# Two edits in a hybrid encoder kernel: the retention scores of two heads in one product over 128 rows, and another way of counting filler products

## The chip, the cores and the metric

The kernel runs on one core of a Trainium2 chip. The metric is the device time of one execution in microseconds (us), the median of several runs. A core has a matrix engine (TensorE, PE in the rows; its weight loads are PEld), a vector engine (VectorE, DVE), a scalar engine (ScalarE, ACT), GpSimd (POOL) and SyncE (SP), each with an instruction stream of its own; semaphores tie them together. All names of tiles in the rows are the program's own.

## What is computed

Two layers of an encoder over 512 prompt frames and 32 sample frames (544 columns, handled as two halves of 272). In every layer four token mixers read one residual stream: stick-breaking attention (sb), retention (ret), forgetting attention (fox) and sparse attention chosen by an indexer (dsa). Their outputs are gated, summed, projected, normalised, and a SwiGLU network follows. The change touches the retention, of which this is the part that matters (four heads of 64):

```
scores = einsum('bnhd,bmhd->bhnm', q, k) * decay[None]
o = einsum('bhnm,bmhe->bnhe', scores, v)
o = o + einsum('bnhd,bhde->bnhe', q, state) * exp((n + 1) * log_gamma)
state = exp(c * log_gamma) * state + einsum('bmhd,bmhe->bhde', k_dec, v)
y_ret = head_norm(o) * silu(g)
```

## The kernel before

Feature-major tiles hold two heads in the 128 partitions: of `q` and `k` (names `rq` and `rk` in the rows, shape 128 x 2 x 544) index p is the pair of heads, and partitions 0 to 63 and 64 to 127 are its heads s = 0 and s = 1. The prompt's 512 frames are taken in four chunks of 128. For each chunk, and for each s, the kernel takes a PSUM bank `z` and multiplies 64 rows of `k` with 64 rows of `q`, once for each pair p (line 1612); VectorE multiplies by the decay into `A` (line 1613). Then come the state (`S`, from the decayed keys `kd`), the product of `S` with the decayed queries `qd`, the product of `A` with the values `rvt`, and a normalisation over each head (`oc`, `st`, `mv`, `rs`). These products are in float32, and TensorE runs each of them as two passes, which are two rows of the trace. The large products (names `wop`, `whi`, `wlo`, `wb` with `T`, `h0hi`, `q`, `yhi`) are split into parts of one pass each.

Order and places are not written by hand. The program is recorded as a list of operations; `Plan.schedule` simulates five engines with estimated durations and lets the operation of the smallest number go first on every engine; `Memory` then assigns SBUF addresses by the times so found, tries four settings (`FITS`) and keeps the one that ends first. An additional tile or another estimated duration can so change addresses, and by them waits and the order, in places far from the edit.

`Plan.fillers` puts filler products into the holes that TensorE has in this plan: a product of 128 columns of the constant tile `idle`, into an unused part of PSUM bank 0 (line 657). They are there to keep TensorE active. Before each operation the number is limited by two things: the hole in front of it less 0.1 us, and what is missing to a share of activity over a trailing stretch (the two constants of `WARM`); a filler counts 0.056 us. The activity of an operation was the time that the plan gives it. All operations are issued at line 659, so the rows carry this line for everything but fillers.

Of the kernel before, what the change touches and what calls it, by code (L numbers as in the profile page):

```python
# [11 lines left out]
F32 = mybir.dt.float32  # L12
F32R = mybir.dt.float32r
BF = mybir.dt.bfloat16
AF = mybir.ActivationFunctionType
OP = mybir.AluOpType
# [5 lines left out]
T = 512  # L22
# [306 lines left out]
class Plan:  # L329
# [305 lines left out]
    def fillers(self, order):  # L635

        share, width = self.WARM
        count, busy, end = {}, [], 0.0
        for i in sorted((i for i in order if self.ops[i].eng == "PE"), key=lambda i: self.ops[i].start):
            op = self.ops[i]  # L640
            s = op.start
            busy = [(a, b) for a, b in busy if b > s - width]
            done = sum(b - max(a, s - width) for a, b in busy)
            n = int(min(share * width - done, s - end - 0.1) / self.IDLE_MM) if end else int(s / 2 / self.IDLE_MM)
            if n > 0:
                count[i] = n
                busy.append((end, end + n * self.IDLE_MM))
            end = s + op.dur
            busy.append((s, end))
        return count  # L650

    def issue(self, order):
# [12 lines left out]
class Build:  # L665
# [875 lines left out]
    def retention(self):  # L1541
        nc, l = self.nc, self.l
        cs = self.fm("cs")
        a, b = CONST_AT["cos"][0], CONST_AT["sin"][1]
        nc.sync.dma_start(cs.rearrange("p a b -> p (a b)"), self.consts_dram[:, a:b])
        q = self.rotary(self.proj(COL["ret_q"], "rq0"), cs)
        k = self.rotary(self.proj(COL["ret_k"], "rk0", 0.125), cs)
# [12 lines left out]
        for c in range(2):  # L1560
            a = COL["ret_g"] + c * 128
            raw = self.load([(self.i["w_in"][l][:, a:a + 128], 0, 128)], 8)
            self.dense(raw, 0, 128, 8, self.hx,
                       lambda h, ps: silu(c, h, ps))
        y = self.fm("y_ret")
        dec = self.const("dec").rearrange("m (s p n) -> m s p n", s=2, p=2)
        qdt = self.const("qdec").rearrange("r (p n) -> r p n", p=2)
        op, os_ = self.outs["ret_state"]
# [36 lines left out]
        for c in range(4):  # L1605
            cc = slice(c * 128, (c + 1) * 128)
            A = self.w512("A", (128, 2, 2, 128))
            for s in range(2):
                r = slice(s * 64, s * 64 + 64)
                z = self.tps("rz")  # L1610
                for p in range(2):
                    nc.tensor.matmul(z[:, p * 128:(p + 1) * 128], k[r, p, cc], q[r, p, cc], start=True, stop=True)
                nc.vector.tensor_tensor(A[:, s], z[:, :256].rearrange("m (p n) -> m p n", p=2), dec[:, s], op=OP.mult)
            kd = kdecay(c * 128, 128, "kdec")
            self.select(SELECT[2])
            N = state_from(S, kd, v[:, c], 128, "g128")
            if c:
                qd = self.w512("qd", (128, 2, 128))
                nc.gpsimd.tensor_tensor(qd, q[:, :, cc], qdt, op=OP.mult)
            o = self.aps("ro")  # L1620
            for p in range(2):
                if c:
                    nc.tensor.matmul(o[:, p * 128:(p + 1) * 128], qd[:, p], S[:, p], start=True, stop=False)
                for s in range(2):
                    h = 2 * p + s
                    nc.tensor.matmul(o[:, h * 64:(h + 1) * 64], A[:, s, p], v[:, c, h * 64:(h + 1) * 64],
                                     start=not c, stop=not c or s == 1)
            self.head_norm_T(o, 128, sg, y, c * 128)
            S = N
# [8 lines left out]
        z = self.tps("rzs")  # L1638
        for p in range(2):
            nc.tensor.matmul(z[:32, p * 64:(p + 1) * 64], k[:, p, T:NT], qb[:, p].rearrange("r s q -> r (s q)"),  # L1640
                             start=True, stop=True)
        A = self.w512("As", (128, 2, 2, 32))
        nc.vector.tensor_tensor(A[:32].rearrange("m p s n -> m s p n"),
                                z[:32, :128].rearrange("m (p s n) -> m s p n", p=2, s=2), dec[:32, :, :, :32],
                                op=OP.mult)
# [5 lines left out]
        o = self.aps("ros")  # L1651
# [436 lines left out]
```

## Time and profile before

| | us |
|---|---|
| median of 3 runs | 1942.51 |
| lowest and highest of them | 1942.05, 1944.62 |
| the profiled execution's own time | 1938.36 |
| its span, first to last instruction | 1936.6 |
| mean granted TensorE clock in the profiled execution | 0.995 of full speed |

A profile page shows one execution: busy time of each engine, a strip of 40 slices, the chain of work that ended last, and groups of equal instructions. Behind it a trace can be asked for single instructions in order of time, for what ended the idle time before one, and for the busy times in chosen stretches. In a timeline row a merged run of equal instructions has one start, one length, a count, and in brackets the idle time before it and the operation that ended it. The length of a product includes its way through the array, so the distance of two starts tells what it occupies, and two lengths that overlap are normal.

### The profile page before, as it was taken

What the parts mean: (1) busy time and instruction counts of PE and PEld (TensorE: products, weight loads), DVE (VectorE), ACT (ScalarE), POOL (GpSimd) and SP (SyncE); (2) the same over time, 40 slices, a digit from 0 to 9 for tenths busy, and PEclk for the clock granted to TensorE, in tenths of its full rate; (3) what the DMA queues carried; (4) which work ended last, traced back from release to release, by engine and by line L of the source; (5) the groups of instructions that cost most, each with busy time, mean ns of one, the idle gap of its engine ahead of it and who ended that gap; (6) DMA issues with size and microseconds to landing.
All of it is one profiled execution on the core that took longest, in us unless ns stands there. A gap on an engine that the chain in (4) does not pass through costs nothing.

```text
span 1936.6 us, 39257 instructions
## 1 busy us (share of the span) xinstructions
PE 1871.6 (97%) x14658; PEld 1815.8 (94%) x14658; DVE 1607.1 (83%) x3566; ACT 1053.3 (54%) x2183; POOL 498.8 (26%) x500
## 2 busy tenths in 40 slices
PE   9999999999999999999999999999999999999997
PEld 8998898999999999999989989999999999999996
DVE  5988768887879989988789796687788799899875
ACT  4465533555637656556465563365556475565552
POOL 0343031143441111321413421312434301114101
PEclk9999999999999999999999999999999999999999
DMA  8222243667542587776413222346665237777741
GB/s 229 79 64 81 55 101 75 153 142 163 145 124 77 135 195 174 170 180 169 130 23 95 60 84 68 78 107 159 151 154 155 86 86 169 188 174 175 171 114 47
DMA packets 387423, 241.38 MB, mean 125 GB/s; under 512 B 27272, under 2 KB 363576, under 8 KB 386976
## 3 DMA queue, kind: packets, MB, share of 16 engines
q1 hardware_dynamic: 361888, 193.78, 36.2%
q0 software_dynamic: 25344, 45.10, 13.8%
q8 instruction: 115, 1.88, 0.4%
q14 instruction: 76, 0.62, 0.1%
HBM read 183.69 MB, written 7.82 MB: 99 GB/s over the span
## 4 chain that ended last, share of the span: by engine, by line
PE 71%; DVE 17%; DMA 5%; ACT 4%; issue 3%; POOL 1%; SPq 1%; POOLq 0%; ACTq 0%; DVEq 0%
PE bank L659 70%; DVE wop L659 3%; DMA ws<-wa 3%; DVE lnw L659 2%; DVE y L659 2%; DVE wsum L659 1%; DVE wlo L659 1%; DVE st L659 1%; DVE q L659 1%; DVE score L659 1%; DVE fu L659 1%; SPq L659 1%; DVE su L659 0%; DVE sv L659 0%; ACT wop L659 0%
## 5 line engine op out<-in xcount | busy, mean ns | idle before, releaser
L659 PE MATMUL bank<-T,wop 128*128 128x272 f32 x3456 | 460.6, 289 | 4.6 <-DVE su L659 3.1
L659 PEld LDWEIGHTS bank<-T,wop 128*128 128x128 f32 x3456 | 443.3, 188 | 7.1 <-DVE su L659 4.3
L659 PE MATMUL bank<-h0hi,wop 128*128 128x272 f32 x1152 | 244.9, 291 | 0.3 <-DVE acc L659 0.3
L659 PEld LDWEIGHTS bank<-h0hi,wop 128*128 128x128 f32 x1152 | 190.0, 188 | 3.6 <-DVE acc L659 0.5
L659 POOL DMA_DIRECT2D wt<-raw x88 | 76.6, 870 | 370.8 <-DVE wop L659 68.2
L659 POOL DMA_DIRECT2D ws<-wa x88 | 76.9, 874 | 352.7 <-DVE wop L659 114.8
L659 ACT ACTIVATE wop<-raw 128x512 fp32r<-128x512 f32 (+1 forms) x176 | 108.9, 620 | 107.1 <-PE bank L659 96.2
L659 PE MATMUL bank<-h0lo,wop 128*128 128x272 f32 x576 | 165.7, 288 | 0.0
L659 PE MATMUL bank<-q,wop 128*128 128x272 f32 x1176 | 153.0, 290 | 4.4 <-DVE su L659 2.6
L659 PEld LDWEIGHTS bank<-q,wop 128*128 128x128 f32 x1176 | 148.8, 189 | 7.5 <-DVE su L659 3.6
L659 DVE TENSOR_TENSOR wop<-raw,wop 128x512 fp32r<-128x512 f32 (+1 forms) x176 | 126.0, 718 | 31.1 <-ACT wop L659 30.5
L659 ACT ACTIVATE wop<-wsum 128x512 fp32r<-128x512 f32 (+1 forms) x176 | 109.1, 620 | 73.7 <-PE bank L659 46.5
L659 PE MATMUL bank<-h0hi,whi 128*128 128x272 f32 (+1 forms) x480 | 146.0, 304 | 2.3 <-ACT h0hi L659 2.3
L659 DVE TENSOR_TENSOR wlo<-raw,whi 128x1024 fp32r<-128x1024 f32 (+1 forms) x92 | 123.7, 1351 | 27.8 <-PE bank L659 12.7
L659 PE MATMUL bank<-h1hi,whi 128*128 128x272 f32 (+1 forms) x480 | 142.3, 296 | 1.1 <-DVE iq L659 1.1
L659 ACT ACTIVATE whi<-raw 128x1024 fp32r<-128x1024 f32 (+1 forms) x92 | 95.5, 1049 | 87.2 <-PE bank L659 46.6
L659 PE MATMUL bank<-h0hi,wlo 128*128 128x272 f32 (+1 forms) x480 | 139.3, 290 | 2.0 <-DVE wlo L659 2.0
L659 PE MATMUL bank<-h0lo,whi 128*128 128x272 f32 (+1 forms) x480 | 139.2, 290 | 2.0 <-DVE h0lo L659 2.0
L659 DVE TENSOR_TENSOR wop<-wsum,wop 128x512 fp32r<-128x512 f32 (+1 forms) x176 | 122.2, 694 | 22.8 <-ACT wop L659 22.0
L659 PE MATMUL bank<-h1lo,whi 128*128 128x272 f32 (+1 forms) x480 | 138.5, 289 | 0.5 <-DVE h1lo L659 0.5
L659 PE MATMUL bank<-h1hi,wlo 128*128 128x272 f32 (+1 forms) x480 | 138.6, 289 | 0.0
L659 PE MATMUL bank<-h1hi,wop 128*128 128x272 f32 x576 | 121.4, 289 | 0.0
(452 smaller groups left out, 5076.7 us busy)
## 6 DMA issues: line engine op xcount, KB each, us to landing
raw<-in_w_in_dram SPq DMA_DIRECT2D x46, 512.0 KB, 3.8
ws<-wa POOLq DMA_DIRECT2D x80, 256.0 KB, 4.4
wt<-raw POOLq DMA_DIRECT2D x80, 256.0 KB, 4.0
raw<-in_w_ffn_in_dram SPq DMA_DIRECT2D x76, 256.0 KB, 3.6
raw<-in_w_in_dram SPq DMA_DIRECT2D x68, 256.0 KB, 3.5
wa<-in_w_ffn_in_dram SPq DMA_DIRECT2D x38, 256.0 KB, 3.5
ws<-in_w_ffn_in_dram SPq DMA_DIRECT2D x38, 256.0 KB, 2.9
wt<-in_w_ffn_in_dram SPq DMA_DIRECT2D x38, 256.0 KB, 4.2
```

Source lines behind the costliest of these rows:

```text
L659: call(*a, **k)
```

## The change

It has two parts. First, a tile `qm` (128 x 2 x 2 x 512, float32) is made once in each layer, after the rotary step: for head s it holds that head's 64 rows of `q` in their own partitions, and zeros in the other 64. GpSimd writes the zeros (two operations), ScalarE copies the rows (two operations). The scores of both heads of a pair are then one product over all 128 rows with 256 columns, and one bank takes all four heads; the multiplication by the decay stays in two operations, which now read this bank. Second, the activity of an operation in `Plan.fillers` becomes the number of its streamed columns over 2400 a microsecond (float32 counts twice) spread over its planned time, in place of that time itself; the limit by the hole and the length of a filler stay.

```diff
         count, busy, end = {}, [], 0.0
+        columns = lambda op: sum((2 if a[1].dtype == F32 else 1) * math.prod(a[0].shape[1:]) for _, a, _ in op.calls)
...
-            busy = [(a, b) for a, b in busy if b > s - width]
-            done = sum(b - max(a, s - width) for a, b in busy)
+            busy = [x for x in busy if x[1] > s - width]
+            done = sum(c * (b - max(a, s - width)) / (b - a) for a, b, c in busy)
...
-                busy.append((end, end + n * self.IDLE_MM))
+                busy.append((end, end + n * self.IDLE_MM, n * 128 / 2400))
             end = s + op.dur
-            busy.append((s, end))
+            busy.append((s, end, columns(op) / 2400))
...
+        qm = self.mem.tile([128, 2, 2, T], F32, name="qm")
+        for s in range(2):
+            r, o = (slice(x * 64, x * 64 + 64) for x in (s, 1 - s))
+            nc.gpsimd.memset(qm[o, :, s], 0.0)
+            nc.scalar.activation(qm[r, :, s], q[r, :, :T], AF.Copy)
...
             A = self.w512("A", (128, 2, 2, 128))
+            z = self.tps("rz")
+            for p in range(2):
+                nc.tensor.matmul(z[:, p * 256:(p + 1) * 256], k[:, p, cc], qm[:, p, :, cc], start=True, stop=True,
+                                 skip_group_check=True)
             for s in range(2):
-                r = slice(s * 64, s * 64 + 64)
-                z = self.tps("rz")
-                for p in range(2):
-                    nc.tensor.matmul(z[:, p * 128:(p + 1) * 128], k[r, p, cc], q[r, p, cc], start=True, stop=True)
-                nc.vector.tensor_tensor(A[:, s], z[:, :256].rearrange("m (p n) -> m p n", p=2), dec[:, s], op=OP.mult)
+                nc.vector.tensor_tensor(A[:, s], z.rearrange("m (p s n) -> m s p n", p=2, s=2)[:, s], dec[:, s], op=OP.mult)
```

In the order of instructions the two parts show as follows. On TensorE in layer 0, at the first chunk's scores, four products of 64 rows stand before; the banks 64 and 65 are the two that scores rotate over, `ident` is the transpose of the keys.

```order
L659 MATMUL bank_60<-h1hi_111,wlo_485 128x272
L659 MATMUL bank_65<-rq_557_444,rk_569_452 128x128 x2
L659 MATMUL bank_64<-rq_557_444,rk_569_452 128x128 x2
L659 MATMUL bank_66<-ident_70,rk_569_452 128x128 x2
L659 MATMUL bank_61<-h0hi_94,wop_542 128x272
L659 MATMUL bank_61<-h0lo_95,wop_542 128x272
```

Now there are two products for the first chunk, and the second chunk's two stand right behind the transpose:

```order
L660 MATMUL bank_60<-h1hi_111,wlo_485 128x272
L660 MATMUL bank_65<-qm_487,rk_569_452 128x256 x2
L660 MATMUL bank_66<-ident_70,rk_569_452 128x128 x2
L660 MATMUL bank_64<-qm_487,rk_569_452 128x256 x2
L660 MATMUL bank_61<-h0hi_94,wop_543 128x272
L660 MATMUL bank_61<-h0lo_95,wop_543 128x272
```

The other score products of the layer follow the same way; the number of runs of score products on TensorE falls. On TensorE in layer 1, between the state product of the second chunk (`kd`) and the product of the state with the queries of the third (`S`, `qd`), large products (`wop`) stand before:

```order
L659 MATMUL bank_66<-rvt_1907,kd_1926 128x128 x2
L659 MATMUL bank_64<-rq_2453_1875,rk_2465_1883 128x128 x2
L659 MATMUL bank_65<-rqb_1950,rk_2465_1883 32x64 x2
L659 MATMUL bank_60<-h0hi_1511,wop_1977 128x272
L659 MATMUL bank_60<-h0lo_1512,wop_1977 128x272
...
L659 MATMUL bank_67<-S_1927,qd_1936 128x128
L659 MATMUL bank_67<-rvt_1907,A_1933 128x64 x2
```

Now the same two stand in a stretch with fillers: 9 ahead of the state product, 32 between it and the product with the queries, and 5 ahead of the next large product.

```order
L660 MATMUL bank_66<-ident_70,rk_2462_1884 128x128 x2
L660 MATMUL bank_65<-rqb_1952,rk_2462_1884 32x64
L658 LDWEIGHTS idle_72
L658 MATMUL bank_60<-idle_72 128x128
...
L660 MATMUL bank_66<-rvt_1908,kd_1928 128x128 x2
...
L660 MATMUL bank_67<-S_1929,qd_1938 128x128
L660 MATMUL bank_67<-rvt_1908,A_1935 128x64 x2
L660 MATMUL bank_66<-ident_70,oc_1934 128x128 x2
```

The large products that filled this place have moved to either side of it. On ScalarE in layer 0, the copies of `qm` are put ahead of the eviction of the sparse attention's weights, `pT`. Before:

```order
L659 ACTIVATE wop_470<-ws_463 128x512
L659 ACTIVATE wop_471<-wsum_468 128x512
L659 ACTIVATE pT_431<-bank_66 128x512
L659 ACTIVATE yhi_530<-y_fox_270 128x1088
L659 ACTIVATE y_dsa_371<-bank_67 64x2x128
```

Now:

```order
L660 ACTIVATE wop_470<-ws_463 128x512
L660 ACTIVATE wop_471<-wsum_468 128x512
L660 ACTIVATE qm_487<-rq_557_444 64x2x512
L660 ACTIVATE pT_431<-bank_66 128x512
L660 ACTIVATE rqb_520<-rq_557_444 64x2x32
```

The first of the two copies stands just ahead of `wop_470`, the second between `wop_471` and `pT_431`; the eviction behind them waits for both.

Over the whole program the fillers rise from 240 to 416. Counted in the new way on the old order there would be 327; so 87 of the 176 more come from the rule, and 89 from work that moved. The places that the prediction speaks of: 9 fillers become 17 at the start of the program, ahead of the first large product; 7 become 32 in the first normalisation's shadow of layer 0's network (ahead of the products of `whi` and `wlo` near 610 us); 17 become 21 and 19 become 21 ahead of products of `q` in the two networks; the others stand in the forgetting attention, in the retention and in the merge. The order of VectorE, ScalarE and TensorE also differs from about the middle of layer 0's stick-breaking attention on, by neighbours that change places.

## Rows read from the trace of the kernel before

**Rows 1.** The page: span; busy time of each engine, its share of the span, its instructions; the chain that ended last, by engine.

```profile
span 1936.6 us, 39257 instructions
PE 1871.6 (97%) x14658; PEld 1815.8 (94%) x14658; DVE 1607.1 (83%) x3566; ACT 1053.3 (54%) x2183; POOL 498.8 (26%) x500
...
PE 71%; DVE 17%; DMA 5%; ACT 4%; issue 3%; POOL 1%; SPq 1%; POOLq 0%; ACTq 0%; DVEq 0%
```

**Rows 2.** Busy times in stretches that hold the retention of layer 0 (first three) and of layer 1 (last two). Columns: stretch, its length, busy time and count of PE, PEld, DVE, ACT, POOL, granted clock, share of the DMA engines, GB/s.

```profile
250.00:266.00 16.00, 13.97 (x112) 12.97 (x111) 9.05 (x17) 5.11 (x11) 7.55 (x8) 1.00 0.09 22
...
285.00:300.00 15.00, 13.80 (x112) 13.07 (x112) 12.75 (x19) 5.44 (x11) 3.65 (x4) 1.00 0.16 44
300.00:318.00 18.00, 15.93 (x135) 13.92 (x131) 16.95 (x58) 3.83 (x10) 2.37 (x4) 1.00 0.47 104
...
1240.00:1262.00 22.00, 21.78 (x169) 20.91 (x168) 18.19 (x36) 6.81 (x14) 5.28 (x7) 1.00 0.34 79
1262.00:1290.00 28.00, 27.14 (x211) 24.64 (x210) 26.04 (x86) 17.54 (x31) 2.94 (x5) 1.00 0.42 96
```

**Rows 3.** Groups of equal instructions: the passes of the score products (busy time of all, mean ns of one, idle time before), and VectorE's multiplication by the decay (shortest, median, longest ns, first and last start).

```profile
L659 PE MATMUL bank<-rq,rk 64*128 64x128 f32 x64 | 10.0, 302 | 0.3 <-DVE rk L659 0.3
...
L659 DVE TENSOR_TENSOR A<-bank,C x16: 388/406/423, 297.0 to 1269.6; 128x256 f32<-128x256 f32 x16
```

**Rows 4.** Timeline of TensorE, layer 0: runs of score passes and the first instruction behind each, and one large product just ahead of a run. Columns: start, length, engine, line, operation, out<-in, form, count.

```profile
293.09 0.72 PE L659 MATMUL bank<-rq,rk 64*128 64x128 f32 x8
293.74 0.44 PE L659 MATMUL bank<-ident,rk 128*128 128x128 f32 x2
...
302.54 0.29 PE L659 MATMUL bank<-T,wop 128*128 128x272 f32 x1
...
302.75 0.71 PE L659 MATMUL bank<-rq,rk 64*128 64x128 f32 x4
303.39 1.02 PE L659 MATMUL bank<-T,wop 128*128 128x272 f32 x6
304.34 0.48 PE L659 MATMUL bank<-rq,rk 64*128 64x128 f32 x2
304.75 0.49 PE L659 MATMUL bank<-S,qd 128*128 128x128 f32 x2
```

**Rows 5.** Timeline of TensorE: the widest float32 product nearby that fills the array's 128 columns, two passes of 288 columns, and what follows.

```profile
215.81 0.73 PE L659 MATMUL bank<-ncks,C 4*128 4x288 f32 x2
216.37 0.28 PE L659 MATMUL bank<-cqs,C 32*128 32x4 f32 x2
```

**Rows 6.** Timeline of TensorE: runs of fillers and what follows them, at the start, in the merge of layer 0 and at its network.

```profile
12.01 0.66 PE L657 MATMUL bank<-idle 128*128 128x128 bf16 x9 [0.75 <-DVE h0lo L659]
12.48 0.37 PE L659 MATMUL bank<-h0hi,whi 128*128 128x272 f32 x1
...
425.68 0.28 PE L657 MATMUL bank<-idle 128*128 128x128 bf16 x2
427.65 0.39 PE L659 MATMUL bank<-yhi,wb 128*128 128x272 f32 x1 [1.68 <-DVE st L659]
...
609.73 0.57 PE L657 MATMUL bank<-idle 128*128 128x128 bf16 x7
610.11 0.37 PE L659 MATMUL bank<-h0hi,whi 128*128 128x272 f32 x1
...
611.78 0.36 PE L659 MATMUL bank<-h0hi,wlo 128*128 128x272 f32 x1 [1.18 <-DVE wlo L659]
```

**Rows 7.** Timelines of VectorE and TensorE: the state of a chunk in layer 1 and the product that waits for it.

```profile
1278.56 0.97 DVE L659 SCALAR_TENSOR_TENSOR S<-S,C,bank 64x64 f32<-64x64 f32 x4 [0.48 <-PE bank L659]
...
1279.39 0.49 PE L659 MATMUL bank<-S,qd 128*128 128x128 f32 x2 [0.86 <-DVE S L659]
```

**Rows 8.** The nearest rows to the operations that make `qm`: a copy on ScalarE and a memset on GpSimd with as many elements a partition (groups; mean ns is the last number before the second bar), and ScalarE's idle time ahead of the eviction that stands behind the copies (timeline).

```profile
L659 ACT ACTIVATE whi<-raw 128x1024 fp32r<-128x1024 f32 (+1 forms) x92 | 95.5, 1049 | 87.2 <-PE bank L659 46.6
...
L659 POOL MEMSET skl<- 64x1024 f32 x4 | 3.8, 948 | 26.0 <-PE bank L659 22.3 <-issue 3.7
...
256.21 0.60 ACT L659 ACTIVATE pT<-bank 128x512 f32<-128x512 f32 x1 [0.95 <-PE bank L659]
```

**Rows 9.** A run of narrow products on TensorE in layer 0 (timeline), and the stretches in which the granted clock was low (columns as in rows 2).

```profile
220.99 3.58 PE L659 MATMUL bank<-pT,vccache_fox_v 128*128 128x32 f32 x24
...
224.40:226.00 1.60, 1.60 (x9) 1.54 (x9) 1.20 (x7) 0.62 (x3) 0.00 (x0) 0.50 0.00 0
226.00:227.70 1.70, 1.70 (x9) 1.70 (x8) 0.48 (x2) 0.90 (x4) 0.00 (x0) 0.50 0.00 0
...
1180.00:1183.00 3.00, 3.00 (x14) 2.83 (x14) 1.09 (x6) 0.42 (x2) 0.00 (x0) 0.52 0.53 156
1183.00:1187.00 4.00, 4.00 (x18) 4.00 (x18) 2.35 (x15) 2.06 (x7) 0.00 (x0) 0.51 0.00 0
```

**Rows 10.** Timeline of TensorE in layer 0's forgetting attention: waits of products and of fillers.

```profile
194.82 0.22 PE L659 MATMUL bank<-bfoxmask,bident 128*128 128x128 bf16 x1 [0.99 <-DVE mx L659]
...
202.28 0.44 PE L657 MATMUL bank<-idle 128*128 128x128 bf16 x5 [1.47 <-DVE dq L659]
202.56 1.13 PE L659 MATMUL bank<-pT,fvt 128*128 128x128 f32 x8
```

## The prediction

> **What bounds the kernel now.** I read the page first. TensorE is busy 97% of the span, VectorE 83%, and 71% of the chain that ended last is TensorE's own work, 17% VectorE's [rows 1]. So a microsecond taken off TensorE is worth something where TensorE is full, and nothing where it waits. Then I read the stretches that the edits lie in. In layer 0 the retention runs from 285 to 318 us: there TensorE is busy 13.80 + 15.93 = 29.73 of 33 us and VectorE 12.75 + 16.95 = 29.70. Both are close to full, and TensorE has 3.3 us idle. In layer 1 (1240 to 1290 us) TensorE is busy 21.78 + 27.14 = 48.92 of 50 us and VectorE 44.23, of which 26.04 lie in the last 28 [rows 2]. So in layer 1 TensorE ends the stage, and in layer 0 the two share it. Last I read the fillers and the granted clock.
>
> **The score products.** The 64 passes of the score products are busy 10.0 us, 0.156 us each [rows 3]. A pass in a run costs less: four take 0.64 us from their start to the next instruction (302.75 to 303.39), two take 0.41, so two more passes cost 0.23, and the rest of some 0.2 us is paid once in a run, on leaving it. On entering one, the large product at 302.54 is followed after 0.21 us, where large products in a run follow each other after about 0.13 (0.29 us rows that overlap); that is 0.08 more [rows 4]. So a run costs about 0.3 us beyond its passes, and in the first chunk eight passes, whose two heads stand side by side, take no longer (0.65 us) than four [rows 4]. The new form has 16 products of 256 columns, two passes each. From below: a pass of 128 float32 columns, 0.115 us, is about two fillers of 128 columns, 0.054 us each [rows 6]; so 256 columns are four of them, 0.217 us, and 32 x 0.217 = 6.9 us. From above, two passes of 288 columns take 0.56 us from start to start, 0.28 each with the entry [rows 5]; for 256 columns that is 0.25, so 32 x 0.25 = 8.0 us. The saving is 2.0 to 3.1 us of TensorE's time; I take 2.6, half in each layer. In layer 1 all of its 1.3 us counts, since TensorE is full there. In layer 0 TensorE waits 3.3 us in the stage anyway, and VectorE's work (16 decays of 0.406 us in all, as many after as before [rows 3]) does not shrink, so I count 0.6 of its 1.3. Sum: -1.9 us, between -3.1 and 0.
>
> The page "TensorE: Matmul & The Clock Gate" of the Trainium skill (Part 3, packing small matmuls) speaks against this edit: products that use different row groups of the array run side by side, so two heads of 64 rows should cost little more than one. The eight passes in 0.65 us agree. By that rule a form that always put both heads side by side would cost eight runs of some 0.73 us, 5.8 us, and the new form would be a loss of 1.6 us (7.4 against 5.8).
>
> The trace shows such neighbours only in part: four passes alone take as long as eight, and most runs before are of four or two.
>
> **The masked queries.** `qm` adds two copies on ScalarE in each layer, 1024 elements a partition, nearest the 1.049 us of `whi`, and two memsets on GpSimd of 0.948 us [rows 8]. From 250 to 266 us ScalarE is busy 5.11 of 16 us and GpSimd 7.55 [rows 2], and the scores begin at 293 us, so the work itself is hidden. What is queued behind the copies is the eviction of `pT`, for which TensorE's next product of the sparse attention waits; ScalarE was idle 0.95 us ahead of it [rows 8]. Two copies of 1.05 in front of it can make it late by up to 2.1 - 0.95 = 1.15 us, in one layer. TensorE has 2.0 us idle in that stretch [rows 2] and large products to do. I take 0, with 1.2 as the upper end. That each decay now waits for all four heads' products (0.85 us in place of 0.64) delays nothing that I can see: the bank is there long before `A` is needed.
>
> **The fillers.** There are 176 more. In a row of seven a filler takes (610.11 - 609.73)/7 = 0.054 us [rows 6], so if nothing covered them they would cost 9.5 us. Most stand ahead of an operation that waits: in the merge the next product came 1.9 us after two fillers, released by VectorE, and three or four more there are free [rows 6]. Three places have no such cover. At 12.01 us nine fillers are followed at once by the first large product [rows 6]; eight more cost 0.43 us. At 609.73 us seven are followed at once, but behind two products TensorE waits 1.18 us for VectorE's `wlo` [rows 6]; 25 more take 1.36, so 0.2 us comes through. The six more in the two networks cost up to 0.3 us. Sum: +0.9 us, between 0 and 9.5.
>
> **The hole in layer 1.** The 46 fillers that now stand in the third chunk's place mark a hole of at least 46 x 0.054 = 2.5 us, where the trace had one wait of 0.86 us for the state [rows 7]. The large products that filled it run elsewhere, and TensorE is full there, so up to 1.6 us comes on top; but VectorE is busy 26.04 of the 28 us there [rows 2] and sets a part of the pace whatever TensorE does. I take +0.8.
>
> **The clock.** Twice the granted clock fell to about 0.5 of full speed, that is the 1.2 GHz level: 224.4 to 227.7 us, and 1180 to 1187. TensorE was busy throughout, but just before the first fall it ran 24 products of 32 columns for 3.58 us [rows 9]. At half speed 3.4 + 6.8 = 10.2 us give 5.1 us of work, so keeping the clock up would gain up to 5.1 us. In the new order the same narrow products stand without a filler among them, since the plan has no hole there. I count 0, with -5.1 as one end; a third such stretch would cost +1.7.
>
> **Sum.** -1.9 + 0 + 0.9 + 0.8 + 0 = -0.2 us on the profiled execution's own 1938.36 us. The median of the runs is 1942.51, 4.15 us above; the same difference gives 1942.3 us.
>
> **The rivals.** (a) Fillers in the way: slower. The rule only knows the planned holes. Where the real hole is shorter, each filler delays the next product by 0.054 us; and a filler writes bank 0, so the first of a run also waits for the last reader of that bank, as at 202.28 us, 1.47 us behind VectorE's `dq` [rows 10]. For it: 416 in place of 240, and 11 runs that begin with such a wait in place of 7. Against it: at 202.28 the next product was barely ready either. If 150 of the 176 stood bare the cost would be 8.1 us in place of 0.9, and the time 1949.5. It decides from 0.2%, 3.9 us, that is from some 90 bare fillers on.
>
> (b) The new order closes waits: faster. In the forgetting attention of layer 0 TensorE waits 0.99 us for `mx` and 1.47 us more at the fillers [rows 10], and neighbours change places there. If that 2.5 us went and the saving of 3.1 counted in full, 1942.5 - 5.6 = 1936.9. Against it: these waits are for VectorE's chain, which has the same work.
>
> (c) The clock stays up: faster. The 5.1 us come back, with the rest of the sum 1937.2. For it: this is where more fillers would help. Against it: none stands where the clock fell.
>
> (d) The row-group rule: had the two heads always shared the array, the edit would cost 1.6 in place of saving 1.9 (-0.2 + 3.5), and the time would be 1945.8. The traces bear it out for one chunk, hardly more.
>
> (e) The edit does not do what it says: a pass of 256 columns takes the 0.28 us of rows 5 and enters and leaves as dearly as a run of 64 rows. Then 32 x 0.28 = 9.0 us against 10.0, a saving of 1.0 and 1943.2 us.
>
> **How the numbers follow.** A measurement of this kernel can tell some 0.2% (3.9 us) from no change. Forecast 0.40, (d) 0.04 and (e) 0.03 lie within it: same 0.47. (b) 0.17 and (c) 0.12: faster 0.29. (a) 0.24: slower. The likeliest is 1942.3 us. The range reaches from 1935.0 (below (b) and (c), where part of both holds) to 1949.5 (all of (a)); it leaves out the full sum of all gains, 1942.5 - 3.1 - 5.1 = 1934.3, and of all costs.
>
> **What would show it.** In the changed profile the score passes should be 32 rows of 128 rows by 256 columns, 6.9 to 8.0 us busy in all, without the 0.2 us behind each run. In layer 1 TensorE should show fillers of some 1.8 us and then the state's product; if VectorE's state comes earlier than their end, (a) is right there. At 12 us the first large product should start 0.43 us later. The stretches at half speed should again follow the narrow products; none at all would mean (c). If the stage of layer 0's forgetting attention is shorter by over 2 us, (b) holds. The forecast is wrong if the sum of fillers followed at once by a product that was ready exceeds 90.

## The result, and the profile after

The changed kernel takes 1954.04 us (median of three runs, 1953.81 to 1958.42) against 1942.51, a ratio of 1.0064 with a 95% interval of 1.0039 to 1.0088: slower by 11.5 us. A second series on another chip (eight runs, below) gave 1953.14 against 1944.85, 1.0042 (1.0024 to 1.0059). The forecast was 1942.3 in a range of 1935.0 to 1949.5.

The profiled execution has its own time of 1958.42, so it is compared with the 1938.36 of the one before: 20.1 us apart (20.0 by the spans). The page:

```profile
span 1956.6 us, 39581 instructions
PE 1891.8 (97%) x14802; PEld 1835.2 (94%) x14802; DVE 1613.3 (82%) x3566; ACT 1056.2 (54%) x2185; POOL 500.7 (26%) x504
...
PE 68%; DVE 18%; DMA 5%; ACT 3%; issue 3%; POOL 1%; SPq 1%; POOLq 0%; ACTq 0%; DVEq 0%
```

Against [rows 1] TensorE is busy 20 us longer, as long as the span has grown; its share of the chain has fallen by 3 points. Its idle time is the same (65.0 us before, 64.8 now), but 176 fillers more, 9.5 us at 0.054, lie in it: idle time and fillers together have grown from 78.0 to 87.3 us (an estimate). No new bottleneck shows; so the stages have to be compared. Busy times in three stages, each from one operation to the same operation (stick-breaking and forgetting attention of layer 0; sparse attention, retention and start of the merge of layer 0; retention of layer 1), with columns as in [rows 2], in the kernel before:

```profile
96.29:207.64 111.35, 106.16 (x848) 99.75 (x847) 94.99 (x258) 71.06 (x155) 41.93 (x29) 1.00 0.27 76
207.64:330.03 122.39, 116.45 (x891) 107.31 (x890) 90.86 (x259) 47.49 (x114) 23.76 (x26) 0.99 0.30 71
...
1237.95:1299.56 61.61, 60.53 (x459) 56.19 (x459) 54.94 (x146) 32.36 (x57) 9.09 (x12) 1.00 0.44 99
```

and in the changed kernel:

```profile
96.15:213.04 116.89, 109.23 (x851) 101.49 (x850) 100.34 (x252) 70.23 (x152) 41.21 (x29) 0.97 0.25 72
213.04:339.91 126.87, 122.38 (x926) 113.65 (x923) 93.36 (x263) 53.57 (x121) 26.71 (x29) 0.96 0.31 72
...
1252.84:1317.12 64.28, 61.36 (x492) 57.85 (x493) 54.54 (x148) 28.00 (x55) 9.35 (x13) 1.00 0.44 98
```

These three are 5.5, 4.5 and 2.7 us longer, and the retention, where the change is written, is only in the last two. In the first, which computes nothing that the change touches, VectorE is busy 5.35 us longer with six instructions fewer. That is the first thing to explain. A part of the first two is the clock (0.97 and 0.96 in place of 1.00 and 0.99). In a second profiled execution of the changed kernel, with a mean clock of 0.994 (the changed kernel again, below), the stages between the same operations take 113.76, 125.48 and 64.25 us, 2.4, 3.1 and 2.6 above before, 8.1 of the 10.5 us by which its span of 1947.1 is longer. So most of the loss lies in these stages. The granted clock has fallen too. The stretches at half clock in the changed kernel (four of seven, and the sum of all; same columns):

```profile
170.71:177.54 6.83, 6.83 (x34) 6.70 (x34) 2.49 (x5) 2.41 (x6) 3.06 (x4) 0.50 0.35 107
232.15:238.98 6.83, 6.83 (x31) 6.70 (x31) 3.38 (x18) 2.21 (x9) 0.00 (x0) 0.50 0.02 5
...
604.20:607.62 3.42, 3.42 (x17) 3.42 (x17) 3.42 (x11) 3.06 (x8) 0.05 (x1) 0.50 0.59 166
...
1194.71:1201.54 6.83, 6.83 (x30) 6.64 (x30) 3.24 (x17) 2.22 (x8) 0.00 (x0) 0.50 0.24 70
sum 34.15, PE 34.15 PEld 33.58 DVE 21.56 ACT 14.29 POOL 7.38; mean PE 4.88 PEld 4.80 DVE 3.08 ACT 2.04 POOL 1.05
```

34.15 us at the 1.2 GHz level against some 10.2 [rows 9], with TensorE busy in all of them: half of the difference, at most 12 of the 20 us between the two profiled executions. (The last 9.0 us of the program before and the last 10.9 of the changed one run at that level too; neither [rows 9] nor the sum counts them.) But the profiled execution before was an unusually lucky one: its mean clock is 0.995, while 106 timed runs of the same kernel, those that the experiments are compared with, had 0.986 to 0.994. The three timed runs of the changed kernel had 0.988 to 0.991, within that, so the 11.5 us between the medians must come mostly from something else.

What the edits themselves did is much as forecast, but for the hole in layer 1. The tile `qm` by its instructions (shortest, median, longest ns), and the score passes in the timeline of TensorE:

```profile
L660 PE MATMUL bank<-qm,rk x32: 377/379/483, 305.5 to 1278.3; 128*128 128x256 f32 x32
...
L660 ACT ACTIVATE qm<-rq x4: 1041/1060/1062, 263.9 to 1230.7; 64x1024 f32<-64x1024 f32 x4
```

```profile
305.47 1.02 PE L660 MATMUL bank<-qm,rk 128*128 128x256 f32 x4
306.33 0.38 PE L660 MATMUL bank<-ident,rk 128*128 128x128 f32 x2
...
312.23 1.08 PE L660 MATMUL bank<-qm,rk 128*128 128x256 f32 x4
312.96 2.98 PE L660 MATMUL bank<-T,wop 128*128 128x272 f32 x21
```

Four passes of 256 columns last 1.02 us with the last one's 0.38, so they start 0.21 us apart, and the next product follows 0.73 to 0.86 us after the first; nothing is paid on leaving, unlike [rows 4]. 32 passes make 6.8 us. The fillers at the three places of the forecast, in the timeline of TensorE:

```profile
12.48 1.11 PE L658 MATMUL bank<-idle 128*128 128x128 bf16 x17 [0.75 <-DVE h0lo L660]
13.40 0.37 PE L660 MATMUL bank<-h0hi,whi 128*128 128x272 f32 x1
...
620.93 1.96 PE L658 MATMUL bank<-idle 128*128 128x128 bf16 x32
622.70 0.37 PE L660 MATMUL bank<-h0hi,whi 128*128 128x272 f32 x1
...
623.36 0.36 PE L660 MATMUL bank<-h0hi,wlo 128*128 128x272 f32 x1 [0.16 <-DVE wlo L660]
...
1282.31 1.95 PE L658 MATMUL bank<-idle 128*128 128x128 bf16 x32
1285.88 0.46 PE L660 MATMUL bank<-S,qd 128*128 128x128 f32 x2 [1.61 <-DVE oc L660]
```

The first product starts 0.92 us behind the first filler in place of 0.47 [rows 6]. At 621 us the row of fillers is 1.39 us longer, and the wait for `wlo` 1.02 shorter (0.16 in place of 1.18). In layer 1's retention the fillers are over 1.6 us before VectorE is ready: they are not in the way; the hole is real, some 3.6 us (1.95 and 1.61) where [rows 7] had a wait of 0.86.

Now the 5.35 us of VectorE. Timeline of the changed kernel, stick-breaking attention of layer 0: VectorE, GpSimd, ScalarE and TensorE.

```profile
114.78 3.46 DVE L660 TENSOR_TENSOR wlo<-raw,whi 128x1024 fp32r<-128x1024 f32 x1
118.27 1.02 DVE L660 SCALAR_TENSOR_TENSOR sa<-bank,st 128x512 f32<-128x512 f32 x2
...
114.61 2.55 POOL L660 TENSOR_TENSOR T_plain<-T_plain,h1lo 128x1088 f32<-128x1088 f32 x1
...
119.00 0.94 ACT L660 ACTIVATE hl<-sa 128x512 fp32r<-128x512 f32 x2 [1.94 <-DVE sa L660]
...
119.68 0.39 PE L660 MATMUL bank<-hl,trin 128*128 128x256 f32 x1 [1.83 <-ACT hl L660]
```

The same operations before:

```profile
114.72 1.02 DVE L659 SCALAR_TENSOR_TENSOR sa<-bank,st 128x512 f32<-128x512 f32 x2 [0.75 <-issue]
115.66 1.22 DVE L659 TENSOR_TENSOR wlo<-raw,whi 128x1024 fp32r<-128x1024 f32 x1
...
107.70 7.62 POOL L659 TENSOR_TENSOR T_plain<-T_plain,h1lo 128x1088 f32<-128x1088 f32 x3
```

Before, VectorE makes `sa` first and `wlo` after GpSimd's additions ended at 115.32; `wlo` takes 1.22 us. Now `wlo` stands ahead of `sa` and starts 0.17 us after GpSimd's second addition, and takes 3.46: it ends 1.08 us after that addition. `sa` comes late behind it, ScalarE waits 1.94 us for `sa`, TensorE 1.83 us for `hl`, where it had no wait before. The profiled executions with this order all have this wait (1.83 us here, 1.83 and 1.84 in the changed kernel again and in the products alone, below). That is what two neighbours that change places cost here. The page "SBUF — State Buffer" of the Trainium skill (SBUF: two separate sides) says it in general: a VectorE operation with two SBUF inputs and a GpSimd operation that reads SBUF share a port that one of them holds for a whole instruction, whoever starts first. These rows agree: 3.46 us beside 1.22.

It is not the only such place. Counting the two-operand operations of VectorE that take at least 1.2 us longer than is usual for their kind, the trace before has 5, and each of these three executions with the new order has 9; in each case an operation of GpSimd runs at the same time.

### The profile page after: what moved, and what is told of

Read it like the earlier page. It is cut to its first block, busy times and chain, and to the rows that moved or that the text cites. A ratio compares the mean times of both kernels' runs of the same rounds, so it can differ in the third digit from the quotient of the medians.

```text
span 1956.6 us, 39581 instructions
## 1 busy us (share of the span) xinstructions
PE 1891.8 (97%) x14802; PEld 1835.2 (94%) x14802; DVE 1613.3 (82%) x3566; ACT 1056.2 (54%) x2185; POOL 500.7 (26%) x504
## 4 chain that ended last, share of the span: by engine, by line
PE 68%; DVE 18%; DMA 5%; ACT 3%; issue 3%; POOL 1%; SPq 1%; POOLq 0%; ACTq 0%; DVEq 0%
PE bank L660 68%; DVE wop L660 3%; DMA ws<-wa 3%; DVE lnw L660 2%; DVE wlo L660 2%; DVE y L660 2%; DVE st L660 1%; DVE q L660 1%; DVE wsum L660 1%; DMA raw<-in_w_ffn_out_dram 1%; DVE score L660 1%; SPq L660 1%; DVE fu L660 1%; DMA xt<-in_x_prompt_dram 0%; DVE sv L660 0%
## 5 line engine op out<-in xcount | busy, mean ns | idle before, releaser
L660 DVE TENSOR_TENSOR wlo<-raw,whi 128x1024 fp32r<-128x1024 f32 (+1 forms) x92 | 130.5, 1427 | 28.9 <-PE bank L660 16.0
```

The source lines that it names most:

```text
L660: call(*a, **k)
```

## The experiments

The planner computes the end of its own simulated schedule for each choice of addresses. Without any address to wait for it gives 1870.8 us before and 1869.8 after: the new products save 1 us in it. With the addresses it gives 1873.9 before and 1879.9 after. So the tile of 8 KB, placed among the others, costs the plan 6 us. That made theory O: the loss is the order and the addresses. Its rivals were F, the fillers stand in the way, and C, the half clock; later T (the tile and the products themselves), P (the products save time) and V (VectorE and GpSimd collide) came in. Each run is compared with the kernel before on the same chip.

**First: the two parts apart, and no fillers.** The rule alone, in the kernel before:

```diff
...
-            done = sum(b - max(a, s - width) for a, b in busy)
+            done = sum(c * (b - max(a, s - width)) / (b - a) for a, b, c in busy)
...
```

> The kernel before with the new filler rule alone: 327 fillers in place of 240, all other work in the old order and at the old addresses. If the loss is the moved order (theory O), this stays within 2 us of before, near 1942.5 us. If fillers stand in the way (theory F), the 87 more cost most of 87 x 0.054 = 4.7 us and the time is 1945 to 1948 us at the mean clock of before (0.993 to 0.995). If the loss is stretches at half clock (theory C) and fillers keep the clock up, it is 1938 to 1943 us with a mean clock no lower than before.

1951.13 against 1943.87 us, 1.0044 (1.0027 to 1.006), mean clock of its runs 0.990 against 0.991. Slower by 7.3: more than all the 87 fillers take (4.7 us at 0.054). O is missed, and C as well, since the clock did not rise; F gives the sign, but not the size. The products alone, with the old rule:

> The changed kernel with the old filler rule: the masked queries, the products of 256 columns and the order and addresses that follow from them, with 252 fillers. Theory O (the new order costs waits): 1950 to 1955 us, most of the 11.5 us. Theory F (fillers in the way): 1941 to 1944 us, near before. Theory C (half clock): slower than before by what its mean granted clock is lower, 1 us for each 0.0005 or so, so 1950 us would go with about 0.991 and 1943 with 0.994.

1955.72, 1.006 (1.0046 to 1.0074), clock 0.988. A little above what O expects, and not F: the first part alone costs 11.9 us. The run has 291 fillers, not the 252 of its expectation; that is 51 more than before, 2.8 us if all stood bare. A part of the 11.9 can be the clock: 0.0028 lower than before (0.9878 against 0.9906), at most 5.5 us of 1950. The two parts do not add up, 7.3 + 11.9 against 8.3 to 11.5 for both. Both kernels without fillers behind the first product:

```diff
-            if n > 0:
+            if n > 0 and not end:
```

> The kernel before without any filler behind the program's first product: all work and order as before. Theory F: the 177 fillers that go were partly in the way, so 1938 to 1942 us at the same mean clock. Theory C with fillers that keep the clock up: more stretches at half clock, mean clock 0.985 to 0.991 and 1948 to 1960 us. Theory O says nothing on fillers: 1942 us.

> The changed kernel without any filler behind the program's first product. Theory F: the whole loss goes, 1941 to 1945 us. Theory O: it stays, 1951 to 1955 us at the clock of the changed kernel (0.988 to 0.991). Theory C with fillers that keep the clock up: 1955 to 1965 us with a mean clock below 0.988; theory C with fillers that do nothing for the clock: about 1953 us with the clock of the changed kernel.

1951.33, 1.0042 (1.0028 to 1.0057), clock 0.984; and 1961.83, 1.0097 (1.0076 to 1.0117), clock 0.981, without one of its six executions, which took 7155.77 us for a reason that the record does not show. The loss of the new order stays without any filler (10.5 us between the two), as O expects and F does not. And fillers do keep the clock up: without them stretches at half clock follow their holes, here in the kernel before without fillers,

```profile
975.30:982.12 6.82, 6.13 (x20) 5.17 (x21) 5.69 (x13) 3.59 (x9) 1.62 (x2) 0.50 0.33 88
1576.04:1582.87 6.83, 6.16 (x27) 6.19 (x28) 6.79 (x19) 4.24 (x10) 0.86 (x1) 0.50 0.49 115
```

at the start of layer 1 and at its network, where the kernel before has

```profile
965.95 2.02 PE L657 MATMUL bank<-idle 128*128 128x128 bf16 x33
...
1562.99 2.02 PE L657 MATMUL bank<-idle 128*128 128x128 bf16 x33
```

in its timeline of TensorE, and no stretch at half clock.

**Second: the order and the addresses without the products.** The masked queries made, but read by the old products:

```diff
...
-                nc.tensor.matmul(z[:, p * 128:(p + 1) * 128], k[r, p, cc], q[r, p, cc], start=True, stop=True)
+                nc.tensor.matmul(z[:, p * 128:(p + 1) * 128], k[r, p, cc], qm[r, p, s, cc], start=True, stop=True)
```

> The masked queries are made as in the changed kernel, but the products are those of 64 rows as before (they read the rows of the masked queries that are not zero), and the filler rule is the old one. So only the tile of 8 KB a partition, its four operations and what they shift in addresses and order are added. The planner's own end of this program is 1876.5 us, against 1873.9 for the kernel before and 1879.9 for the changed one. Theory O (the moved addresses and order cost what the planner's end says): before + 2.5 us, 1945 to 1948 us. If the tile and its copies alone were the cost (theory T): as slow as the run with products only, 1950 to 1956 us. If the products of 256 columns were the cost: 1943 to 1944 us, as before.

1959.03 against 1943.99, 1.009 (1.0073 to 1.0107): 15 us, with not one new product in it. So a loss of this size needs no new product; but O's size is missed by far, and T's range (1950 to 1956) by 3 us. The masked queries chunk by chunk:

```diff
-        qm = self.mem.tile([128, 2, 2, T], F32, name="qm")
...
+            qm = self.mem.tile([128, 2, 2, 128], F32, name="qm")
```

> The products of 256 columns with the old filler rule, but the masked queries are made chunk by chunk in tiles of 2 KB in place of one of 8 KB. Planner's end 1877.2 us. Theory O: before + 3.2 us, 1945 to 1949 us, so 5 to 9 us faster than the run with products only. Theory T: 1943 us if the size of the tile is what costs. If the products of 256 columns were the cost: 1951 to 1956 us as with products only.

1948.51, 1.0027 (1.0007 to 1.0046), as O expects. And the kernel before itself at two other settings of its planner:

```diff
-FITS = ((10.0, 5.0), (5.0, 5.0), (10.0, 2.0), (10.0, 10.0))
+FITS = ((10.0, 5.0),)
```

> The kernel before, nothing changed but that the planner's first setting for addresses is used in place of the third, which it had chosen. Planner's end 1875.2 in place of 1873.9 us. Theory O: 1944 to 1947 us. Theory T, and any theory in which the products or the tile are the cost: 1943 to 1944 us.

> The kernel before with the planner's fourth setting for addresses, whose end is 1885.6 in place of 1873.9 us, the same work in another order. Theory O: before + 8 to 14 us, 1952 to 1958 us, with no masked queries in it at all. Theory T: 1943 to 1945 us.

1947.45, 1.0024 (1.001 to 1.0037), and with (10.0, 10.0) 1962.73, 1.0094 (1.0078 to 1.011). The same work, other addresses: 3.5 and 18.7 us, with no masked queries. So T is not needed; the run with halves, below, takes it away.

**Third: the product with the order held, a good place for the tile, and the collisions.** The old products' program of the second group, with each product over 128 rows, in the same order at the same addresses:

```diff
-                nc.tensor.matmul(z[:, p * 128:(p + 1) * 128], k[r, p, cc], qm[r, p, s, cc], start=True, stop=True)
+                nc.tensor.matmul(z[:, p * 128:(p + 1) * 128], k[:, p, cc], qm[:, p, s, cc], start=True, stop=True)
```

> The same program as the run with masked queries and old products, operation by operation in the same order, at the same addresses and with the same fillers; only each score product now reads all 128 rows, masked queries included, in place of 64 rows. So the shape of the product is tried with the order held. Theory P (the products save what the rows say, 64 passes of 0.107 us without the 0.2 us behind each run, some 2.7 us of TensorE's time, and part of that reaches the end): 1 to 3 us faster than that run. If the products of 128 rows were what made the changed kernel slow: several us slower than that run.

1950.38 against 1942.11, 1.0034 (1.0013 to 1.0054), where the old products had 1.009: the two intervals don't meet, and the products of 128 rows are faster, by more than P expected. How much of this is the products, the traces show. They have the same operations in the same order on TensorE, and around the score products of each layer, from one operation to the same, 64 rows take (columns as in [rows 2])

```profile
298.55:316.40 17.85, 16.64 (x125) 14.29 (x124) 16.08 (x47) 4.31 (x10) 2.84 (x4) 1.00 0.33 75
1258.69:1276.60 17.91, 16.70 (x128) 14.63 (x127) 16.56 (x46) 6.54 (x14) 2.65 (x3) 1.00 0.40 86
```

and 128 rows

```profile
299.38:315.62 16.24, 15.10 (x124) 14.38 (x123) 15.62 (x46) 4.41 (x10) 2.64 (x4) 1.00 0.34 82
1261.57:1278.53 16.96, 15.80 (x127) 14.86 (x126) 16.36 (x46) 6.54 (x14) 2.65 (x3) 1.00 0.36 82
```

That is 1.6 and 0.9 us, 2.5 in all, as P expected. The rest of the difference between the runs is not the products: all 64 passes together were busy 10.0 us [rows 3]. A part of it can be the clock (0.988 in the run with 64 rows, 0.9905 in this one). TensorE's timeline with 64 rows:

```profile
308.82 0.71 PE L659 MATMUL bank<-qm,rk 64*128 64x128 f32 x4
309.46 1.02 PE L659 MATMUL bank<-T,wop 128*128 128x272 f32 x6
```

and with 128:

```profile
309.30 0.71 PE L659 MATMUL bank<-qm,rk 128*128 128x128 f32 x4
309.77 1.00 PE L659 MATMUL bank<-T,wop 128*128 128x272 f32 x6
```

From the first pass to the next large product 0.47 us in place of 0.64: the 0.17 us on leaving are gone, as the forecast had it. The masked queries in two tiles of 4 KB, at a setting where the planner's end is low:

```diff
-FITS = ((10.0, 5.0), (5.0, 5.0), (10.0, 2.0), (10.0, 10.0))
+FITS = ((10.0, 3.0),)
...
+            if c % 2 == 0:
+                qm = self.mem.tile([128, 2, 2, 256], F32, name="qm")
```

> The products of 256 columns with the old filler rule, the masked queries in two tiles of 4 KB for two chunks each, and the planner's setting (10, 3) for addresses. Chosen because the planner's own end of it, 1871.7 us, lies 2.2 us below that of the kernel before (1873.9) and 8.2 below that of the changed one (1879.9). Theory O (addresses and order, as the planner's end has them): 1938 to 1943 us, 12 to 16 us faster than the run with products only. Theory T (the masked queries or the products cost): 1950 us or more.

1941.27 against 1942.11, 0.9996 (0.9983 to 1.001). The same products that cost 11.9 us in one order cost nothing in another. This is the strongest run for O. Then the large additions of GpSimd replaced by fills (the sums are left out), in the order before and in that of the products alone:

```diff
+                if self.ops[i].eng == "POOL" and call.__name__ == "tensor_tensor" and math.prod(a[0].shape[1:]) > 1000:
+                    x0 = k["out"] if "out" in k else a[0]
+                    call, a, k = self.real.gpsimd.memset, (x0 if x0.dtype == F32 else x0.bitcast(F32), 0.0), {}
                 call(*a, **k)
```

> The kernel before in its own order, with the large additions that GpSimd makes from SBUF (over 1000 elements a partition, the sums of the strip products, some 2.5 us each) replaced by a fill of their result with zeros, 1 us. Left out are those sums, nothing else. Theory V (the changed order makes VectorE's two-operand work and GpSimd's additions collide): 1 to 4 us faster than before, VectorE's stretched operations in the attention of layer 0 go. If collisions don't matter: as before.

> The run with products only, in its own order, with the same additions replaced by fills. Theory V: the gap of 10 to 12 us to the kernel before falls to 3 to 6 us against the kernel before without these additions, since the three or four operations of VectorE that took 3.2 to 3.8 us in place of 1.2 no longer do. If the order costs through other waits (buffers that come free later): the gap stays at 8 us or more.

1934.96, 0.9955 (0.9937 to 0.9972), and 1938.40, 0.9973 (0.9955 to 0.999): the gap between the two orders falls from 11.9 to 3.4 us, inside what V expected, and the order before gains 7.2 as well, more than expected. Not all of the fall need be the stretched operations themselves: without the additions both orders have the same clock (0.9915), where the products only had 0.988 against 0.991, at most 5.5 us of the 11.9. Whether the waits that went also kept the clock up is not shown. In the new order without the additions, at the place shown above:

```profile
113.23 1.21 DVE L662 TENSOR_TENSOR wlo<-raw,whi 128x1024 fp32r<-128x1024 f32 x1
114.47 1.02 DVE L662 SCALAR_TENSOR_TENSOR sa<-bank,st 128x512 f32<-128x512 f32 x2
...
116.36 0.39 PE L662 MATMUL bank<-hl,trin 128*128 128x256 f32 x1
```

`wlo` still stands ahead of `sa`, but takes 1.21 us, and TensorE doesn't wait for `hl`. None of VectorE's operations is stretched by 1.2 us any more, in either order, where the orders had 9 and 5. A fill is also shorter than an addition, so what waits for GpSimd itself gains in both; that part is not told apart.

The stretched operations explain the order of the changed kernel, but not all slow orders. The run with masked queries and old products (15.0 us) has 5 of them and that with (10.0, 10.0) (18.7 us) has 4, no more than the kernel before, and VectorE is busy 1601.2 and 1606.6 us there, not longer than its 1607.1. One of them, `ikl` of 3.29 us at 45 us, is followed in both by a wait that the trace before does not have, here with masked queries and old products:

```profile
48.19 0.65 PE L659 MATMUL bank<-ikl,iq 128*128 128x256 f32 x2 [2.82 <-DVE ikl L659]
```

What the rest of their loss is stays open.

**Fourth: what the filler rule costs.** In the order with halves:

> The masked queries by halves, whose order is as fast as that of the kernel before, with the new filler rule: the same order and addresses, 323 fillers in place of 241. Theory F (added fillers stand in the way and give the clock little): 2 to 7 us slower than the same program with the old rule, 1943 to 1948 us, at a mean clock no higher than its 0.990. Theory C (they keep the clock up): 1936 to 1941 us at a mean clock of 0.992 or more.

1944.70 against 1944.85, 1.0000 (0.9985 to 1.0014), against 0.9996 with the old rule: 82 more fillers cost nothing that can be measured, and the clock (0.990) is the same. That is neither the 2 to 7 us that F expects against the old rule nor C's gain. The changed kernel again:

> The changed kernel again, unchanged, beside the kernel before on this chip: how far it is from the run with products only (291 fillers, 1955.7 us, 11.9 above before) in more runs. If the 125 fillers that it has more cost what the two traces show (5.2 us of full-speed time) and give back 3 us of clock, it is 12 to 15 us above before; if they pay, it is below 10.

1953.14, 1.0042 (1.0024 to 1.0059), 8.3 us above before; its eight runs have a mean clock of 0.9905, as the kernel before (0.991). With the products only it was 11.9 at 0.988. So here the 125 more fillers pay, if anything, and the loss of the changed kernel in these runs is not the clock. Last, the rule with fewer fillers, and the rule without the additions:

```diff
-            n = int(min(share * width - done, s - end - 0.1) / self.IDLE_MM) if end else int(s / 2 / self.IDLE_MM)
+            n = int(min(share * width - done, s - end - 0.6) / self.IDLE_MM) if end else int(s / 2 / self.IDLE_MM)
```

> The kernel before with the new filler rule, but a hole must be 0.6 us longer than its fillers in place of 0.1: 281 fillers at 27 places in place of 327 at 28, the order and addresses of before. Theory F: at least half of the 7.3 us that the rule alone cost is gone, 1943 to 1947 us. Theory C (fillers keep the clock up, more is better): slower than with the rule alone, above 1951 us. If the cost of the rule alone was the luck of its runs: no change against it.

> The kernel before with the new filler rule (327 fillers, old order), and the same large additions of GpSimd replaced by fills as in the two runs without additions; left out are those sums. Theory V (the rule costs because fillers shift work by a few tenths of a microsecond, and VectorE and GpSimd then meet in another order): within 2 us of the kernel before without additions, 1933 to 1937 us or 0.9945 to 0.9965 of before. If the rule costs by itself (its fillers, or the clock): 5 to 8 us more than that run, 1940 us or more.

1953.21 against 1944.85, 1.0044 (1.0028 to 1.006), with 281 fillers: no better than with 327. F falls: it is not the number of fillers. The traces agree: fillers that are followed at once by the next product are 170 before, 214 with the rule alone and 173 here, for the same loss. Nor is it, where it can be compared, a wait for bank 0: with the rule alone, fillers at 301, 992 and 1432 us wait 1.45, 1.08 and 1.28 us ahead of their product, and in the kernel before the product itself waits there 1.20, 1.08 and 1.25 us. And 1941.72 against 1943.94, 0.9982 (0.9967 to 0.9997), 5.2 us above the run without additions in the old rule (0.9955 to 0.9982): V is missed, and the rule costs by itself, as the other expectation said. The difference of 2 us to the 7.3 is within the intervals. One place shows how little it takes to move a meeting of the two engines. Kernel before, VectorE and GpSimd in the sparse attention of layer 0, timeline:

```profile
271.00 3.22 DVE L659 TENSOR_TENSOR xs<-xs,cs 128x1088 f32<-128x1088 f32 x1
274.14 0.68 DVE L659 TENSOR_TENSOR wop<-wsum,wop 128x512 fp32r<-128x512 f32 x1
...
270.54 2.53 POOL L659 TENSOR_TENSOR rk<-rk,cs 128x1088 f32<-128x1088 f32 x1 [1.21 <-DMA xs<-rk]
```

The rule alone, the same operations and the product that waits:

```profile
274.87 1.29 DVE L660 TENSOR_TENSOR xs<-xs,cs 128x1088 f32<-128x1088 f32 x1 [0.97 <-DMA xs<-rk]
276.12 3.00 DVE L660 TENSOR_TENSOR wop<-wsum,wop 128x512 fp32r<-128x512 f32 x1
...
274.91 3.66 POOL L660 TENSOR_TENSOR rk<-rk,cs 128x1088 f32<-128x1088 f32 x1 [2.64 <-DMA xs<-rk]
...
280.84 0.65 PE L660 MATMUL bank<-T,wop 128*128 128x272 f32 x3 [0.96 <-DVE su L660]
```

The order is the same; the transfer `xs<-rk`, which both engines need, took 4.0 us from issue to landing in place of 2.4. Before, GpSimd is first by 0.46 us and `xs` is stretched, `wop` is free; now VectorE is first by 0.04 us, GpSimd's addition grows to 3.66, and `wop` meets it. TensorE waits 0.96 us, where it had no wait. Most of that is the transfer, for which VectorE stood 0.97 us; its two operations together take 4.29 us in place of 3.90. So what the rule alone costs is open: its runs have a clock lower by about 0.001, which is at most 2 us, and no cause is shown for the other 5.

## Why the prediction was wrong

**The step that failed** is rival (b) with the term that it stood for: that the new order could only close waits, "these waits are for VectorE's chain, which has the same work". The work is the same, but not its duration: an operation of VectorE that meets an addition of GpSimd takes 3.46 us in place of 1.22, and there are 9 such in place of 5. A changed order had no loss in the sum beyond 0.8 us for the hole in layer 1. Its price is 11.9 us (products only, some of it clock), and four other orders cost 3.5 to 18.7. Idle time and fillers of TensorE, which the sum had 1.7 us longer (0.9 and 0.8), are 9.3 longer. In the planner's own numbers the new order had 6 us, in the same direction. The meetings with GpSimd account for 3 to 8.5 of the 11.9 us, according to how much of the clock is counted with them (11.9 falls to 3.4 without the additions, and up to 5.5 of it can be clock); for the two slowest of the other orders their number is no explanation, and what those lose stays open.

**The products**: right. 32 passes at 0.21 us are 6.8 us of TensorE's time, the low end that was given (6.9), and the 0.2 us on leaving are gone; as a group the passes are busy 8.8 us, above the 6.9 to 8.0 that were named as a sign. With the order held, products of 128 rows take 2.5 us less in the two stages; 2.6 of TensorE's time were forecast. Rivals (d) and (e) are out.

**The masked queries**: right. The copies take 1.06 us (1.05 forecast), and none of the products waited for `qm`. What they cost came with the new order and addresses, not with their work.

**The fillers**: near in the two places that were read (0.45 us at the start against 0.43; 1.39 less 1.02, so 0.37, at the network against 0.2). As a sum they cannot be given: 0.9 was forecast, and the runs show 7.3 more in the old order, nothing in the order with halves, and 3.6 less in the changed kernel's (with intervals that overlap). Fillers followed at once by the next product are 74 more than before, so the sign of over 90 did not show. Rival (a) has the right sign of the result for a reason that the run with fewer fillers takes away.

**The hole in layer 1**: too small. Its fillers stand ahead of a wait of 1.61 us, so they are free; but the hole is 3.6 us, not 2.5, and the stage is 2.7 us longer at full clock (2.6 in the second profiled execution), where the terms gave -0.5. This too is the moved order.

**The clock**: the forecast was made from one execution that was luckier than most (0.995 against 0.986 to 0.994), and added the 4.15 us to the median without asking what they were. No case changed its sign by that, but up to 12 of the 20 us between the two profiled executions are such luck. Of the seven stretches at half clock in the changed kernel two begin behind runs of 13 to 15 products of 32 columns, as was forecast (at 232.15 and 1194.71 us); the others stand elsewhere.

**The range** ended at 1949.5, the whole of rival (a); no bound had been set for a moved order, which [rows 10] could not give. The stage of the forgetting attention, which had to be over 2 us shorter for rival (b), is 2.4 to 5.5 us longer.

## What to carry to other kernels

Where a planner sets order and addresses, an added tile is a new draw: measure the edit with the order held, or at several placements, before its own cost is argued. Look for operations of VectorE and GpSimd with operands in SBUF that come near each other, count how many are stretched, and count in both ways who comes first; but do not put every slow order down to them. A profile is one execution: compare its clock with that of the timed runs before a sum is set on it.

## What was not expected of the hardware

A lead of 0.04 us in place of a lag of 0.46 decided which operation of VectorE was stretched, and whether GpSimd's addition was (3.66 us in place of 2.53). Stretches at half clock came at other places in each execution of nearly the same program, some behind products of 32 columns, some at or behind waits of TensorE of 1 to 3 us (1.96 us ahead of the one at 675.88 us in the changed kernel; 2.5 and 2.7 us at the two shown above without fillers). Single runs of the kernel before lie between 1937.8 and 1952.8 us, the longer ones mostly at the lower clocks. Fillers of 0.054 us do prevent some of them: without the fillers the mean clock fell from 0.991 to 0.984, and the time rose by 7.5 us.
